# Finer regions in the kernel's own order planner: quarters of the inverse's tiles, halves of stored and output weights, single table columns

## The chip, the cores and the metric

The kernel runs on one core of a Trainium2 chip. The metric is the device time of one execution in microseconds (us), as the median over several runs; lower is better.

## The reference, cut to what matters

One layer of a decoder trunk works on 4096 positions of width 1024. The input is normalised (RMSNorm) and multiplied by one input projection. Its columns feed two groups of heads: four heads of gated linear attention, and eight heads of RWKV-7 time mixing with a delta rule. Both outputs are gated, concatenated to 1024 columns, multiplied by an output projection, added to the input and normalised again. The step that matters here is the recurrence of the RWKV heads:

```python
sa = jnp.einsum('bhvk,bhk->bhv', S, -kk_t)
S = (S * w_t[:, :, None, :]
     + sa[..., None] * (kk_t * a_t)[:, :, None, :]
     + v_t[..., None] * k_t[:, :, None, :])
y = jnp.einsum('bhvk,bhk->bhv', S, r_t)
```

The kernel does it in chunks of 64 positions. Within a chunk each position depends on all earlier ones, so each chunk and head needs the inverse of a unit triangular 64x64 matrix.

## The kernel before, in words

**Tiling.** The 4096 positions are cut into 8 blocks of 512. For each block the kernel projects the normalised input tile by tile (29 weight tiles of 1024x128, each kept as a high and a low fp16 half, three products per tile), does the two head groups, and then the output projection (8 more weight tiles). The weights are split into their halves on the chip at the start and stored to DRAM (`wdr`, one tensor for each of the 37 tiles); later blocks load the halves again with `get_w` (L612).

**A unit.** The RWKV heads go in pairs: 4 pairs by 8 blocks are 32 units, numbered 0 to 31. `rwkv_ab` (L862) prepares a unit. It writes the masked triangular matrices into the tile `Nb` (VectorE, COPY_PREDICATED), and then inverts the 32x32 diagonal blocks of all chunks and heads at once. Their rows have to be laid out differently for that, so they go through DRAM twice, by copies on SP's queue: four copies `nd<-Nb` (one for each 32 partitions of `Nb`), four copies `f<-nd` (each fetches the whole of `nd` into another 32 partitions of the tile `f`, named `f4` in the code), then 31 steps of two TENSOR_TENSOR each that build the inverse in `Tc` (on GpSimd; on VectorE for unit 31 alone), four copies `td<-Tc`, and four copies `Nb<-td`, each into the 32x32 blocks of one quarter of `Nb`. `rwkv_i` (L1012) then transposes blocks of `Nb` into `Ta` and completes the 64x64 inverse with TensorE. `rwkv_c` (L1034) is the serial chain over the 8 chunks, three dependent matmul pairs each (`ch<-sv,DD`, `ch<-us,Nb`, `ch<-uv,bk`). `out_last` (L1306) is the output projection of the last block.

**What sets the order.** The kernel writes its program order itself. Every instruction is first recorded as a `Step` with a modelled duration (`put`, L223), and the order in which the streams of work hand in their steps comes from a first running estimate (`account`, L169). `parts` (L105) says which regions an operand covers for estimated times, `whole` (L203) which regions it covers for the edges between steps. If two steps touch a region with the same key, a write after a write, a read after a write or a write after a read makes an edge, and mostly a delay too. A copy that writes a region another copy has just written is therefore modelled as starting after that one has landed. Before the change a DRAM tensor is one region, an on-chip tile is two (partitions 0 to 63 and 64 to 127), and a table of scalars (`scl`, `invs`, `pkt` and others) is one. `forward` (L264) and `backward` (L332) then schedule the steps as lists, for five pairs of parameters ten times each, and the program is written out in the order of the schedule with the shortest modelled end. Each engine, and SP with its copies, executes its instructions in that order. The semaphores are put in afterwards by the framework, from the real addresses and not from these keys.

The edges of a copy come from these lines of `put`:

```python
if k in wlast:
    s.follow(wlast[k], got(wlast[k]) if timed and eng != "T" else None)
for m in readers.get(k, ()):
    s.follow(m, (0.95 + SPARE if m.eng == "D" else 0.1) if timed else None)
```

Of the kernel before, what the change touches and what calls it, by code (L numbers as in the profile page):

```python
# [11 lines left out]
F16 = mybir.dt.float16  # L12
# [6 lines left out]
DRAM = bass.MemoryType.DRAM  # L19

P = 128
DM = 1024
KT = 8
# [23 lines left out]
NC = TB // C  # L47
# [34 lines left out]
def hymba_kernel(ctx, tc, xT, wt, wg, wo, wua, gup, pk, ck, out):  # L82
# [14 lines left out]


    TABLES = ("pkt", "scl", "invs", "hinv", "mu_s", "omu_s", "carry", "wosc", "woinv", "gnh", "lnh")
    HEADS, XS = set(), set()  # L100
    now = [0.0]
    streams = []
    ready, used, busy = {}, {}, {}

    def parts(ap):  # L105
        if ap.tensor.name == out.tensor.name or ap.tensor.name.rsplit("_", 1)[0] in TABLES:
            return []
        if ap.space == DRAM:
            return [(ap.tensor.name, 0)]
        a = ap.start_partition()  # L110
        hs = range(a // 64, (a + ap.shape[0] - 1) // 64 + 1)
        if ap.tensor.name in HEADS:
            o = ap.offset % P // 64
            e = range(2) if ap.ap[-1][1] > 64 else range(o, o + 1)
            return [(ap.tensor.name, h, i) for h in hs for i in e]
        if ap.tensor.name in XS:
            o = ap.offset % (4 * TB) // TB
            e = range(o, o + max(1, math.prod(ap.shape[1:]) // TB)) if ap.dtype == F16 else range(4)
            return [(ap.tensor.name, h, 2 + i) for h in hs for i in e]
        return [(ap.tensor.name, h) for h in hs]  # L120
# [48 lines left out]
    def account(eng, out, ins, d, lag, cols=0, tiles=None):  # L169
        rdy = lambda k: (lambda r: r[0] + early(r[1], eng))(ready.get(k, (0.0, "")))  # L170
        t = max([0.0] + [rdy(k) for a in ins for k in parts(a)]
                + [used.get(k, 0.0) for k in parts(out)]
                + [rdy(k) for k in parts(out) if eng != "T"])
        if eng == "T":
            t0, d = array.put(max(t, now[0]), d, cols, tiles)
            t, now[0] = t0, array.free
        else:
            if eng == "D":
                t0 = place("H", t, 0.5)
                t = t0 + 1.15  # L180
            t = place(eng, t, d)
            if eng != "D":
                t0 = t
        for a in ins:
            for k in parts(a):
                used[k] = max(used.get(k, 0.0), t + d + (0.95 if eng == "D" else 0.1))
        for k in parts(out):
            ready[k] = (t + d + lag, eng)
        return t0
# [13 lines left out]
    def whole(ap):  # L203
        if ap.tensor.name == out.tensor.name:
            return []
        if ap.tensor.name.rsplit("_", 1)[0] in TABLES or ap.space == DRAM:
            return [(ap.tensor.name, 0)]
        return parts(ap)

    class Step:  # L210
# [12 lines left out]
    def put(t0, eng, d, lag, cols, tiles, tab, outs, ins, f):  # L223

        keys = lambda aps: {k: k in {y for x in aps for y in parts(x)} for a in aps for k in whole(a)}
        ki, ko = keys(ins), keys(outs)
        for k in list(ki) + list(ko):
# [250 lines left out]
    def sb(pool, shape, dt, tag, bufs=1):  # L478

        key = (tag, dt)  # L480
        if key not in ring:
            ring[key] = [0, [pool.tile(shape, dt, tag=f"{tag}_{i}", name=f"{tag}_{i}") for i in range(bufs)]]
        r = ring[key]
        t = r[1][r[0] % len(r[1])]
        r[0] += 1
        return t
# [32 lines left out]
    for g in range(4):  # L519
        q = slice(32 * g, 32 * g + 32)  # L520
# [38 lines left out]
    Nb = [sb(un, [P, NC, 192], F32, f"Nb{i}") for i in range(NBUF)]  # L559
# [37 lines left out]
    wdr = [dr.tile([2, P, KT, P], F16, tag=f"wdr{i}", name=f"wdr{i}") for i in range(NWT + KT)]  # L597
# [987 lines left out]
```

## Time and profile before

| what | value |
|---|---|
| median of 3 runs | 2355.93 us (2353.73 to 2357.6) |
| the profiled execution's own time | 2350.84 us |
| its span, from the first to the last instruction | 2348.7 us |
| TensorE busy | 2230.6 us |
| VectorE, ScalarE, GpSimd busy | 1715.9, 1257.4, 865.6 us |
| mean granted TensorE clock | 0.982 |
| GpSimd waiting for the copies `f<-nd` | 468.1 us |

PE is TensorE, DVE is VectorE, ACT is ScalarE, POOL is GpSimd, SP is SyncE, whose queue (SPq) issues the copies. Nearly every instruction is put down to L438, the planner's helper that writes it out, so groups are told apart by their tiles: `bank<-x,wr` is a matmul that writes a PSUM bank from the tiles `x` and `wr`. The rows of a timeline give start, duration, engine, operation, tiles, how many instructions were merged, and in brackets how long the engine had been idle and what ended that. The wait lists give the engine with what it was about to do, what it waited for, the total in us, how many times, and the longest. The table of windows gives for each stretch its length, then busy time and instructions of PE, PEld (weight loads), DVE, ACT and POOL, the granted clock, the DMA engines' busy share and GB/s.

### The profile page before, as it was taken

What the parts mean: (1) busy time and instruction counts of PE and PEld (TensorE: products, weight loads), DVE (VectorE), ACT (ScalarE), POOL (GpSimd) and SP (SyncE); (2) the same over time, 40 slices, a digit from 0 to 9 for tenths busy, and PEclk for the clock granted to TensorE, in tenths of its full rate; (3) what the DMA queues carried; (4) which work ended last, traced back from release to release, by engine and by line L of the source; (5) the groups of instructions that cost most, each with busy time, mean ns of one, the idle gap of its engine ahead of it and who ended that gap; (6) DMA issues with size and microseconds to landing.
All of it is one profiled execution on the core that took longest, in us unless ns stands there. A gap on an engine that the chain in (4) does not pass through costs nothing.

```text
span 2348.7 us, 52029 instructions
## 1 busy us (share of the span) xinstructions
PE 2230.6 (95%) x19304; PEld 1365.0 (58%) x19304; DVE 1715.9 (73%) x3801; ACT 1257.4 (54%) x3229; POOL 865.6 (37%) x2212
## 2 busy tenths in 40 slices
PE   6998999899999999999999999999999999999976
PEld 2555565456665557556575556655575565755643
DVE  7977778568773886849776687748867487766756
ACT  7557765345643646545654556446464555544442
POOL 2442333524334153444524253341524446241300
PEclk9988999999999999999999999999999999999989
DMA  5685645354334642445434543346424464344432
GB/s 183 199 267 167 187 151 151 93 175 139 111 105 128 191 147 74 127 128 188 131 92 124 184 145 109 106 127 192 148 76 128 121 193 121 98 119 123 123 96 75
DMA packets 275362, 325.41 MB, mean 139 GB/s; under 512 B 131572, under 2 KB 132772, under 8 KB 275108
## 3 DMA queue, kind: packets, MB, share of 16 engines
q1 hardware_dynamic: 275108, 322.10, 45.5%
q8 instruction: 151, 2.47, 0.4%
q14 instruction: 103, 0.84, 0.1%
HBM read 276.94 MB, written 45.05 MB: 137 GB/s over the span
## 4 chain that ended last, share of the span: by engine, by line
PE 72%; DVE 14%; DMA 7%; ACT 4%; issue 2%; SPq 1%; POOL 0%; DVEq 0%; ACTq 0%; POOLq 0%
PE bank L438 63%; PE ch L438 7%; PE y L438 3%; DVE DD L438 1%; DMA wg<-wdr 1%; SPq L438 1%; DVE bk L438 1%; DVE x L438 1%; DMA rn<-bcda 1%; DVE nta L438 1%; DMA xr<-in_xT_dram 1%; ACT wo L438 1%; DVE Nb L438 1%; DMA wdr<-wo 1%; DVE mgr L438 1%
## 5 line engine op out<-in xcount | busy, mean ns | idle before, releaser
L438 PE MATMUL bank<-x,wr 128*128 128x512 f16 x3264 | 795.7, 381 | 13.3 <-DVE SC L438 4.7
L438 POOL TENSOR_TENSOR tm<-Tc,f 128x60 f32<-128x60 f32 (+24 forms) x961 | 338.3, 352 | 583.1 <-DMA f<-nd 468.1
L438 PEld LDWEIGHTS <-wr 128*128 128x128 f16 x3264 | 314.1, 100 | 314.7 <-issue 25.6
L438 POOL TENSOR_TENSOR Tc<-Tc,tm 128x60 f32<-128x60 f32 (+24 forms) x961 | 356.7, 371 | 74.6
L438 PE MATMUL bank<-x,wg 128*128 128x512 f16 x1536 | 376.9, 381 | 1.9 <-ACT bk L438 1.2
L438 PE MATMUL bank<-x,wo 128*128 128x512 f16 x1488 | 364.2, 382 | 2.2 <-DMA wr<-wdr 0.8
L438 DVE SCALAR_TENSOR_TENSOR sv<-ch,PC,psd 64x64 f32<-64x64 f32 x448 | 126.5, 282 | 217.2 <-PE ch L438 212.1
L438 POOL TENSOR_TENSOR xacc<-xacc,xr 128x512 f32<-128x512 f32 x98 | 132.7, 1354 | 344.2 <-ACT xr L438 229.5
L438 PEld LDWEIGHTS <-wg 128*128 128x128 f16 x1536 | 147.7, 100 | 149.3 <-issue 8.1
L438 PEld LDWEIGHTS <-wo 128*128 128x128 f16 x1488 | 146.2, 101 | 133.5 <-issue 4.9
L438 PE MATMUL bank<-wg,x 128*128 128x128 f16 x3072 | 197.5, 222 | 12.4 <-DMA wg<-wdr 12.3
L438 PEld LDWEIGHTS <-x 128*128 128x128 f16 x3120 | 189.6, 100 | 32.3 <-issue 20.0
L438 ACT ACTIVATE psd<-sv,PC 128x128 f32<-128x128 f32 x256 | 102.3, 400 | 180.7 <-DVE sv L438 135.2
L438 ACT COPY uv<-ch 64x64 f32<-64x64 f32 x512 | 105.8, 207 | 106.7 <-PE ch L438 100.8
L438 POOL MEMSET Tc<- 32x8 f32 (+1 forms) x160 | 23.6, 148 | 360.1 <-DMA td<-Tc 312.2
L438 ACT COPY us<-ch 64x64 f32<-64x64 f32 x512 | 105.5, 206 | 91.7 <-PE ch L438 83.5
L438 PEld LDWEIGHTS ch<-sv,DD 128*128 128x128 f32 x512 | 91.5, 192 | 41.4 <-DVE sv L438 14.9
L438 PEld LDWEIGHTS ch<-uv,bk 128*128 128x128 f32 x512 | 91.1, 192 | 41.5 <-ACT uv L438 16.1
L438 PEld LDWEIGHTS ch<-us,Nb 128*128 128x128 f32 x512 | 88.6, 192 | 44.7 <-ACT us L438 21.5
L438 ACT ACTIVATE sa<-bank,mu_s 128x512 f32<-128x512 f32 x104 | 71.6, 688 | 75.1 <-PE bank L438 74.3
L438 PE MATMUL ch<-uv,bk 128*128 128x128 f32 x512 | 105.8, 289 | 5.5 <-ACT uv L438 5.2
L438 PE MATMUL ch<-sv,DD 128*128 128x128 f32 x512 | 105.2, 288 | 4.9 <-DVE sv L438 4.7
(333 smaller groups left out, 3681.7 us busy)
## 6 DMA issues: line engine op xcount, KB each, us to landing
wr<-wdr SPq DMA_DIRECT2D x256, 256.0 KB
wg<-wdr SPq DMA_DIRECT2D x184, 256.0 KB
xr<-in_xT_dram SPq DMA_DIRECT2D x176, 256.0 KB
wo<-wdr SPq DMA_DIRECT2D x128, 256.0 KB
f<-nd SPq DMA_DIRECT2D x128, 128.0 KB
x<-in_wt_dram SPq DMA_DIRECT2D x29, 512.0 KB
wdr<-wo SPq DMA_DIRECT2D x25, 512.0 KB
out_dram<-mgg SPq DMA_DIRECT2D x33, 256.0 KB
```

The source lines that it names most:

```text
L438: put(t0, self.name, d, lag, cols, tiles, tab, outs, ins, lambda: f(*a, **kw))
```

## The change

The change edits only the two functions that give regions their keys. No instruction is added or removed by it, and no operand or tile changes; the edges and delays that the planner works with do.

- `dram`, new, splits three kinds of DRAM tensor. `nd` has four regions: a copy `nd<-Nb` touches one, a copy `f<-nd` all four. `td` has four: a copy `td<-Tc` touches one, a copy `Nb<-td` all four. Each `wdr` has two, the high and the low half of a weight.
- `FINE` gives `Nb` a region for every 32 partitions and `f` one for every 16, in place of one for every 64. So the four copies into `f` no longer share a key, and neither do the four into `Nb`.
- The tile `wo` (the output weights, and the staging tile of the weight split) gets a region for each half, when an fp16 operand touches one half only.
- `whole` gives a table one region for each column in place of one for the table.

```diff
+    FINE = {"Nb": 32, "f": 16}
...
+    def dram(ap):
+
+        name = ap.tensor.name
+        if name.startswith("nd"):
+            return [(name, i) for i in (range(4) if ap.shape[0] == 32 and len(ap.shape) == 2 else [ap.offset // (NC * 1024) % 4])]
+        if name.startswith("td"):
+            return [(name, i) for i in (range(4) if ap.ap[0][0] >= 1024 else [ap.offset // 1024 % 4])]
+        if name.startswith("wdr"):
+            return [(name, i) for i in ([ap.offset // (P * DM) % 2] if ap.ap[0][1] == P and len(ap.shape) == 3 and ap.shape[1] == KT and ap.shape[2] == P else range(2))]
+        return [(name, 0)]
+
     def parts(ap):
         if ap.tensor.name == out.tensor.name or ap.tensor.name.rsplit("_", 1)[0] in TABLES:
             return []
         if ap.space == DRAM:
-            return [(ap.tensor.name, 0)]
+            return dram(ap)
         a = ap.start_partition()
+        tag = ap.tensor.name.rsplit("_", 1)[0].rstrip("0123456789_")
+        if tag in FINE:
+            q = FINE[tag]
+            return [(ap.tensor.name, h) for h in range(a // q, (a + ap.shape[0] - 1) // q + 1)]
         hs = range(a // 64, (a + ap.shape[0] - 1) // 64 + 1)
+        if tag == "wo":
+            o = ap.offset // DM % 2
+            e = range(o, o + 1) if ap.dtype == F16 and ap.ap[1][0] < DM else range(2)
+            return [(ap.tensor.name, h, i) for h in hs for i in e]
...
     def whole(ap):
...
-        if ap.tensor.name.rsplit("_", 1)[0] in TABLES or ap.space == DRAM:
-            return [(ap.tensor.name, 0)]
+        if ap.space == DRAM:
+            return dram(ap)
+        if ap.tensor.name.rsplit("_", 1)[0] in TABLES:
+            w = math.prod(ap.tensor.shape[1:])
+            return [(ap.tensor.name, i) for i in range(ap.offset % w, ap.offset % w + math.prod(ap.shape[1:]))]
         return parts(ap)
```

## The prediction

> **What bounds the kernel now.** I read the page first, then a table of windows, then the waits of PE by window, and last the timelines of the place where the waits are.
>
> ```profile
> PE 2230.6 (95%) x19304; PEld 1365.0 (58%) x19304; DVE 1715.9 (73%) x3801; ACT 1257.4 (54%) x3229; POOL 865.6 (37%) x2212
> ...
> PE   6998999899999999999999999999999999999976
> ```
>
> PE is the bound, and its tenths are below 9 almost only in the first and the last slices. The windows say how much is lost where:
>
> ```profile
> 0.00:235.00 235.00, 194.63 (x1527) 116.04 (x1528) 190.72 (x528) 153.50 (x297) 84.93 (x178) 0.93 0.65 204
> 235.00:470.00 235.00, 219.14 (x1813) 132.05 (x1811) 172.28 (x393) 136.30 (x369) 91.62 (x266) 0.98 0.49 146
> 470.00:2232.00 1762.00, 1732.96 (x15264) 1067.09 (x15263) 1280.36 (x2680) 926.41 (x2444) 688.31 (x1763) 1.00 0.44 132
> 2232.00:2349.00 117.00, 83.85 (x707) 49.84 (x705) 72.49 (x201) 41.17 (x121) 0.74 (x5) 0.88 0.30 86
> ```
>
> The second number after the stretch is PE's busy time. PE is idle for 40.4 us of the first 235, 15.9 us of the next, 29.0 us of the long middle (98.4% busy there) and 33.2 us of the last 117. An edit that changes only the order can win no more than these idle times, and the time that the lower clock (0.93 and 0.88, the column before the last two) costs beside them. The waits of PE, first for the tail, then for the stretch from 235 to 2232, then for the head:
>
> ```profile
> PE bank L438 <- DVE Ta L438: 12.3, 3, 11.5
> ```
>
> ```profile
> PE bank L438 <- DMA wg<-wdr: 12.8, 7, 3.6
> ...
> PE bank L438 <- DVE Ta L438: 2.0, 3, 0.8
> ```
>
> ```profile
> PE ch L438 <- ACT uv L438: 3.1, 4, 1.5
> PE ch L438 <- DVE sv L438: 2.8, 5, 0.7
> ...
> PE ch L438 <- ACT us L438: 1.9, 3, 1.1
> ```
>
> One wait stands out: 11.5 us in the tail for `Ta`, the transposed blocks of the inverse that `rwkv_i` takes from `Nb`. The timelines of PE, DVE and SP show it:
>
> ```profile
> 2252.30 0.31 PE L438 MATMUL bank<-Ta,Nb 32*32 32x32 f32 x2 [11.54 <-DVE Ta L438]
> ```
>
> ```profile
> 2241.01 0.19 DVE L438 TENSOR_TENSOR tm<-Tc,f 128x31 f32<-128x31 f32 x1
> ...
> 2251.82 0.42 DVE L438 STREAM_TRANSPOSE Ta<-Nb 32x256 f32<-32x256 f32 x1
> ...
> 2256.98 0.17 DVE L438 TENSOR_TENSOR Tc<-Tc,tm 128x8 f32<-128x8 f32 x1
> ...
> 2274.37 0.90 DVE L438 STREAM_TRANSPOSE Ta<-Nb 32x256 f32<-32x256 f32 x2
> ```
>
> ```profile
> 2219.84 2.18 SPq L438 DMA_DIRECT2D nd<-Nb  x4
> 2223.52 0.30 SPq L438 DMA_DIRECT2D td<-Tc  x1
> ...
> 2231.46 0.31 SPq L438 DMA_DIRECT2D f<-nd  x1
> 2231.83 0.41 SPq L438 DMA_DIRECT2D td<-Tc  x1
> 2232.28 0.45 SPq L438 DMA_DIRECT2D f<-nd  x1
> ...
> 2233.72 0.42 SPq L438 DMA_DIRECT2D td<-Tc  x1
> 2234.20 0.90 SPq L438 DMA_DIRECT2D f<-nd  x2
> ...
> 2237.99 0.46 SPq L438 DMA_DIRECT2D td<-Tc  x1
> ...
> 2241.36 1.02 SPq L438 DMA_DIRECT2D Nb<-td  x2
> ...
> 2244.45 0.96 SPq L438 DMA_DIRECT2D Nb<-td  x2
> ...
> 2257.22 1.80 SPq L438 DMA_DIRECT2D td<-Tc  x4
> ```
>
> Two units are in flight. The `td` copies from 2223.5 to 2238.0, the `Nb` copies and the transposes at 2251.8 belong to unit 30; the `nd` and `f` copies and the VectorE steps from 2241.0 to 2257.2 to unit 31, the last. Unit 30's inverse was there at 2223.5, when its first `td` copy went out, but the fourth went out 14.5 us later. That is the planner's doing: four copies with one key are planned each after the last has landed, and SP takes what the plan put between. The chip asks for no such thing. At 2257.22 four `td` copies go out in 1.80 us, and at 2219.84 four `nd` copies in 2.18 us, less than one copy's way to DRAM and back (3.4 us and more from the last `td` issue at 2237.99 to the first `Nb` copy). The real semaphores know the quarters already.
>
> **The change part by part.** No instruction is added or removed, so busy times stay; what can move is idle time.
>
> *Quarters of `nd`, `td`, `f` and `Nb`, the tail.* For unit 30 the last `td` copy moves from 2238.0 to 2223.5 + 3/4 of 1.80 = 2224.9, 13.1 us earlier, and two more us are won where the `Nb` copies no longer go in spaced pairs (2241.36 to 2245.42 is 4.1 us, four in a row about 2.0). `Ta` then comes at about 2251.8 - 15 = 2237, ahead of the end of PE's work at 2252.3 - 11.5 = 2240.8. The whole wait of 11.5 us goes. What is late next is unit 31: its chain follows unit 30's. Its transposes stand at 2274.4, 17 us after its inverse ended at 2257.2. Its `f` copies can go out some 3.4 us after 2222.0, at 2225.4 where the first now goes at 2231.5, so 6 us earlier; the VectorE steps need 16 us, and behind them four `td` and four `Nb` copies take 1.80 + 3.4 + 2.0 = 7.2 us to issue; with 6.4 us from the last `Nb` issue to `Ta` (2245.4 to 2251.8 for unit 30) that is 13.6 in place of 17.2. So unit 31 moves by 6 + 3.6 = 10 us if VectorE starts as soon as `f` allows, and by up to 15 if the plan also takes out the gap ahead of 2241.0. PE is not idle through all of that: behind the wait it runs at a lower clock.
>
> ```profile
> 2232.00:2252.00 20.00, 8.76 (x49) 4.04 (x47) 13.34 (x51) 3.30 (x8) 0.74 (x5) 0.85 0.55 130
> 2252.00:2290.00 38.00, 34.48 (x340) 22.93 (x341) 21.14 (x63) 20.40 (x63) 0.00 (x0) 0.86 0.28 80
> ```
>
> 38 us at 0.86 lose 5.3 us at the most. The tail is therefore worth 10 us (unit 31 is late next) to 17 us (wait and clock both gone); I take 12, near the wait itself.
>
> *The same, the head.* Unit 0 shows the same spread, here by its first `td` copy, its last one, and POOL's wait until it could clear `Tc` for the next unit:
>
> ```profile
> 139.48 0.48 SPq L438 DMA_DIRECT2D td<-Tc  x1
> ...
> 153.50 0.43 SPq L438 DMA_DIRECT2D td<-Tc  x1
> ```
>
> ```profile
> 158.72 0.90 POOL L438 MEMSET Tc<- 128x256 f32 x5 [24.66 <-DMA td<-Tc]
> ```
>
> About 12 us go from that chain. What PE lost to the first chains are the three waits of `ch` above, 7.8 us. DVE is busy for 190.7 of the 235 us there with the weight split, so an earlier chain may only find PE idle at another time. Between 0 and 8 us, I take 3.
>
> *The same, the middle.* POOL's waits for `f` and `td` shrink there too, but POOL has time to spare. PE's 29 us of idle time over 1762 hold hardly any wait for the inverse (2.0 us for `Ta` above). The order is worked out anew as a whole, and its effect here isn't known. The trace bounds it by its own stretches of 235 us, the worst and the best of the middle:
>
> ```profile
> 470.00:705.00 235.00, 229.16 (x2094) 144.42 (x2093) 180.34 (x375) 126.00 (x328) 85.05 (x212) 0.99 0.44 132
> ...
> 1645.00:1880.00 235.00, 233.34 (x2074) 141.22 (x2071) 163.63 (x355) 124.07 (x324) 101.63 (x275) 1.00 0.41 118
> ```
>
> With 7.5 stretches like the best (1.66 us idle) the middle has 12.4 us idle in place of 29, a gain of 17; with all like the worst (5.84) 43.8, a loss of 15. I take 0, as it stands.
>
> *Halves of `wdr` and `wo`, columns of the tables.* The loads of the two output halves need no longer be planned one after the other, but in no window is a wait of PE for them among the rows that matter; the large one is for `wg`, whose halves are tiles of their own already. Cover: the loads go out a projection ahead; without it each could cost what a wait for `wg` costs, 12.8 / 7 = 1.8 us. The stored halves and the columns matter while the weights are split, where they only allow other orders. I take 0 for these, and the bounds are those of the head (0 to -8, and as much the other way, since a worse order costs what a better one wins).
>
> *A rule that speaks against packing.* The trace gives 3.4 us from the last spread `td` issue to the first `Nb` copy. By the Trainium skill (DMA: Bandwidth & Descriptors, Queues, rings and completion order) the write that signals a copy's end lands only behind every earlier write of the same DMA engine, also of other queues; a packed group behind large loads would then be signalled later. No row here separates that. If it cost each of unit 30's and unit 31's second round trips one more us, the tail would be worth 10 instead of 12.
>
> *Sum.* -12 - 3 + 0 + 0 = -15 us against the profiled execution: 2350.84 - 15 = 2335.8. That execution is 5.1 us below the median of the runs shown, so for the median 2355.9 - 15 = **2341 us**.
>
> **Rivals.**
>
> *A. More of the same.* Tail 17, head 8: 2355.9 - 25 = 2331 us. For it speaks the clock of 0.86; against it unit 31, which is late next, and the busy VectorE of the head.
>
> *B. No change.* The tail's gain is given back: unit 31's inverse on VectorE isn't moved, since the last block's other VectorE work stands ahead of 2241.0, or the middle loses as much as the tail wins. A mere 0 to 4 us remains: 2354 us. That the edit doesn't act at all is part of this, but the four-fold copies above are all planned by the keys it splits.
>
> *C. Packed copies hold up weight loads (slower).* SP issues in order. Today weight loads stand between the spread copies; four packed copies are 1.8 us of issue, and the first copy of the next group waits for the last of the one before, with the loads behind it in the queue. In the middle, at 98.4% busy, PE has no slack for a late weight, and `wg<-wdr` is its largest wait already: 1.8 us a time. One more such wait in every second unit is 16 x 1.8 = 29 us, less the 15: 2370 us. It decides from 9 more waits on (15 / 1.8 = 8.3). Against it: a load goes out when its buffer is free, a projection ahead, and packed groups let SP go sooner.
>
> **How the numbers follow.** This kernel's measurement can tell about 0.2%, 4.7 us, from no change. Chances: forecast (2331 to 2350) 0.45, A 0.12, B 0.10, C 0.33. Faster is the forecast and A, 0.57; the same is B, 0.10; slower is C, 0.33. The range goes from the forecast with the middle's best (2341 - 15 = 2326) to C as priced, 2370; below it lies a small part of A, above it some two fifths of C (more late weights than one in every second unit). The forecast's own range is 2331 to 2350.
>
> **What would show it.** POOL's wait for the `td` copies, over the whole run, is the sum that the spread makes:
>
> ```profile
> POOL Tc L438 <- DMA td<-Tc: 312.2, 24, 24.7
> ```
>
> Right: `nd`, `f`, `td`, `Nb` copies of one unit go out in fours within about 2 us; PE's wait of 11.5 us for `Ta` after 2240 is gone and the window of the last 117 us has some 12 us less idle time; POOL's total wait for `td<-Tc` (312 us) falls by a third or more; the middle's PE share stays near 98.4%. Wrong: the copies are still spread, or PE's waits for `wg<-wdr` and `wr<-wdr` grow above some 28 us (C), or the middle's idle time grows by more than the tail's shrinks.

## The result, and the profile after

The changed kernel takes 2329.2 us (median of 4 runs, 2324.2 to 2333.7), the kernel before 2356.8 us (median of 4). The ratio is 0.988, with a 95% interval of 0.986 to 0.991: faster by 27.5 us, where 15 were forecast. The profiled execution took 2324.2 us, with a span of 2322.4; the one of before 2350.84 and 2348.7. The profiled execution of one kernel further down (the kernel before with the constant 0.44) ran in a slow state, at a mean granted clock of 0.56, so only the times of its other runs are used.

The work is the same; what has moved is where PE stands idle and how fast its clock runs. Here is the first part of the page of the kernel after:

```profile
PE 2221.9 (96%) x19304; PEld 1368.5 (59%) x19304; DVE 1720.4 (74%) x3801; ACT 1246.0 (54%) x3229; POOL 878.7 (38%) x2212
```

PE's busy time falls by 8.7 us although it has the same 19304 matmuls; a part of that is the mean granted clock, which rose from 0.982 to 0.985. The copies did what was expected. This is SP's timeline of the kernel after for the last two units:

```profile
2191.85 2.38 SPq L461 DMA_DIRECT2D td<-Tc  x4
...
2195.58 1.94 SPq L461 DMA_DIRECT2D Nb<-td  x4
2200.28 1.78 SPq L461 DMA_DIRECT2D nd<-Nb  x4
2203.40 1.71 SPq L461 DMA_DIRECT2D f<-nd  x4
...
2229.62 1.84 SPq L461 DMA_DIRECT2D td<-Tc  x4
...
2233.92 1.78 SPq L461 DMA_DIRECT2D Nb<-td  x4
```

Each group of four goes out in about 2 us here; over all units most do, though half of the `nd` groups still take longer, up to 7.9 us. Unit 30's way back (`td` to the last `Nb`) takes 5.7 us where it took 21.9. Over the 32 units, from SP's whole timeline, the median way out (first `nd` issue to the end of the last `f` issue) falls from 16.2 to 7.2 us, the median way back from 15.6 to 6.6. In the waits of the whole run, POOL waits less than half as long for `td`, and more for `f`, since it now comes back earlier and stands idle ahead of its next unit instead:

```profile
POOL tm L461 <- DMA f<-nd: 675.1, 30, 48.9
POOL Tc L461 <- DMA td<-Tc: 139.4, 30, 15.6
```

**Where the time came from.** The two tables of windows, of before and then of after, have the same stretches at the start, and the last 117 us of each span at the end:

```profile
0.00:118.00 118.00, 92.45 (x664) 50.81 (x666) 97.31 (x273) 77.26 (x138) 43.11 (x72) 0.96 0.60 190
118.00:235.00 117.00, 102.19 (x867) 65.23 (x866) 93.42 (x256) 76.24 (x160) 41.82 (x107) 0.89 0.70 218
...
2231.70:2348.70 117.00, 84.15 (x708) 49.99 (x706) 72.49 (x201) 41.17 (x122) 0.74 (x5) 0.88 0.30 86
```

```profile
0.00:118.00 118.00, 91.54 (x664) 51.57 (x664) 98.05 (x273) 79.13 (x141) 50.26 (x85) 0.97 0.64 203
118.00:235.00 117.00, 109.08 (x955) 69.09 (x952) 102.93 (x277) 81.58 (x179) 40.60 (x116) 0.98 0.74 225
235.00:470.00 235.00, 225.83 (x1963) 138.25 (x1961) 171.35 (x405) 138.13 (x375) 95.18 (x254) 1.00 0.52 151
470.00:2205.40 1735.40, 1702.91 (x15001) 1055.26 (x15003) 1273.50 (x2640) 904.25 (x2411) 692.65 (x1759) 0.99 0.46 133
2205.40:2322.40 117.00, 92.58 (x738) 54.34 (x732) 74.56 (x208) 42.86 (x126) 0.00 (x0) 0.85 0.28 82
```

A stretch costs PE its idle time, and at most (1 - clock) x length for running slowly; I call the sum the lost time. It counts the time twice in which PE idles at the low clock, so it is an upper estimate. From 118 to 235 us before lost 14.8 + 12.9 = 27.7 us, after 7.9 + 2.3 = 10.3. Over the first 470 us (the row from 235 to 470 of before stands in the prediction) it is 78.5 before and 49.4 after: 29 us won, give or take 2 for the rounding of the clock. With the low clock counted only where PE is busy, from the trace's own record of the clock, it is 23 us. By 470 us the kernel after has done 3582 matmuls, the kernel before 3344. The last 117 us lost 46.9 before and 42.0 after: 5 us won, by either count. The span is 26.3 shorter, so the middle lost some 8 us.

**The head, seen closer.** Unit 0's way back, in SP's timelines of before (its first `td` copy, at 139.48, stands in the prediction) and then of after, and the first link of its chain that needs the inverse, in PE's timelines of both:

```profile
161.67 1.32 SPq L438 DMA_DIRECT2D Nb<-td  x2
```

```profile
130.99 1.94 SPq L461 DMA_DIRECT2D td<-Tc  x4
...
135.82 1.85 SPq L461 DMA_DIRECT2D Nb<-td  x4
```

```profile
172.07 0.33 PE L438 MATMUL ch<-us,Nb 128*128 128x64 f32 x2
```

```profile
143.94 0.33 PE L461 MATMUL ch<-us,Nb 128*128 128x64 f32 x2
```

The `nd` copies of unit 0 start at the same time in both (80.2 and 80.5 us), but this link comes 28 us earlier: 8 us are won on the way out up to the start of the inverse (101.25 and 93.69 us), and 20 between the first `td` copy and the first matmul on `Ta` (28.8 us before, 8.4 after). The windows of before, while the chain of unit 0 ran, and of after, for the same chain and then the same time:

```profile
176.00:205.00 29.00, 20.81 (x114) 13.06 (x114) 21.07 (x60) 26.57 (x64) 13.31 (x28) 0.76 0.64 197
```

```profile
186.00:191.00 5.00, 2.81 (x13) 1.58 (x11) 4.38 (x10) 4.69 (x13) 4.29 (x10) 1.00 0.00 0
191.00:204.70 13.70, 8.48 (x46) 6.25 (x46) 8.03 (x33) 13.04 (x35) 0.35 (x2) 0.50 0.72 221
```

```profile
143.00:176.00 33.00, 30.07 (x183) 16.87 (x184) 27.05 (x77) 27.12 (x60) 18.46 (x51) 1.00 0.83 260
176.00:205.00 29.00, 25.13 (x333) 18.41 (x333) 25.52 (x68) 23.24 (x58) 0.74 (x5) 1.00 0.76 221
```

Before, the first chain came late, at 172 us, and from 186 us on PE had little else left to do. PE stood idle between the links, and from 191 to 204.7 us the granted clock was 0.50 (the 0.76 is the mean with the 1.00 ahead of it). There the links took twice as long, as these two matmuls of PE's timeline of before show:

```profile
182.09 0.39 PE L438 MATMUL ch<-uv,bk 128*128 128x128 f32 x2
...
192.64 0.80 PE L438 MATMUL ch<-uv,bk 128*128 128x128 f32 x2 [1.52 <-ACT uv L438]
```

After, the chain starts at 144 us, among projections, and the clock stays at 1.00.

**The tail, seen closer.** The wait of 11.5 us for `Ta` is gone. What came in its place is in PE's timeline of after and the window around it:

```profile
2223.70 0.43 PE L461 MATMUL ch<-us,Nb 128*128 128x64 f32 x2 [0.93 <-ACT us L461]
...
2230.00 0.80 PE L461 MATMUL ch<-sv,DD 128*128 128x128 f32 x2 [0.84 <-DVE sv L461]
...
2234.86 0.80 PE L461 MATMUL ch<-uv,bk 128*128 128x128 f32 x2 [2.79 <-ACT uv L461]
...
2240.21 1.49 PE L461 MATMUL bank<-x,wo 128*128 128x512 f16 x3
```

```profile
2222.00:2240.00 18.00, 10.19 (x63) 7.36 (x62) 14.76 (x45) 9.76 (x33) 0.00 (x0) 0.61 0.41 88
```

Unit 30's chain now runs earlier, but alone. The output projection that could fill its gaps (`bank<-x,wo`) comes at 2240, behind the scaling of the last block. These 18 us lose 7.8 of idle time and at most 7.0 of clock. It is a bare chain in place of a bare wait.

The chain could have gone on 12 us sooner, while PE still had projections to do. Its first three matmul pairs are done on PE at 2209.7, but VectorE's next step for it (`sv<-ch`) comes only at 2221.5, behind the steps of unit 31's inverse, which VectorE runs from 2209.7 on:

```profile
2209.28 0.38 PE L461 MATMUL ch<-uv,bk 128*128 128x128 f32 x2
```

```profile
2209.72 0.19 DVE L461 TENSOR_TENSOR tm<-Tc,f 128x31 f32<-128x31 f32 x1
...
2221.53 0.27 DVE L461 SCALAR_TENSOR_TENSOR sv<-ch,PC,psd 64x64 f32<-64x64 f32 x1
```

### The profile page after: what moved, and what is told of

Same layout as the page of the kernel before. It is cut to its first block, busy times and chain, and to the rows that moved or that the text cites. A ratio compares the mean times of both kernels' runs of the same rounds, so it can differ in the third digit from the quotient of the medians.

```text
span 2322.4 us, 52066 instructions
## 1 busy us (share of the span) xinstructions
PE 2221.9 (96%) x19304; PEld 1368.5 (59%) x19304; DVE 1720.4 (74%) x3801; ACT 1246.0 (54%) x3229; POOL 878.7 (38%) x2212
## 4 chain that ended last, share of the span: by engine, by line
PE 67%; DVE 16%; DMA 8%; ACT 4%; issue 2%; SPq 2%; POOL 0%; DVEq 0%; ACTq 0%; POOLq 0%
PE bank L461 58%; PE ch L461 6%; PE y L461 3%; SPq L461 2%; DMA xr<-in_xT_dram 2%; DVE DD L461 2%; DVE nta L461 1%; DMA wdr<-wo 1%; DVE x L461 1%; DVE Nb L461 1%; DVE bk L461 1%; DVE mgr L461 1%; DVE xr L461 1%; DVE mgg L461 1%; DMA rn<-bcda 1%
## 5 line engine op out<-in xcount | busy, mean ns | idle before, releaser
L461 POOL TENSOR_TENSOR tm<-Tc,f 128x60 f32<-128x60 f32 (+24 forms) x961 | 352.4, 367 | 758.3 <-DMA f<-nd 675.1
L461 POOL TENSOR_TENSOR Tc<-Tc,tm 128x60 f32<-128x60 f32 (+24 forms) x961 | 351.0, 365 | 74.4
L461 PEld LDWEIGHTS <-x 128*128 128x128 f16 x3120 | 189.8, 100 | 24.2 <-issue 12.9
L461 PEld LDWEIGHTS ch<-sv,DD 128*128 128x128 f32 x512 | 92.2, 192 | 40.1 <-DVE sv L461 10.8
L461 PE MATMUL ch<-us,Nb 128*128 128x64 f32 x512 | 91.4, 260 | 8.2 <-ACT us L461 8.0
```

Of the source, the lines that this page charges most:

```text
L461: put(t0, self.name, d, lag, cols, tiles, tab, outs, ins, lambda: f(*a, **kw))
```

## The experiments

Three theories. **Q**: shorter round trips of the inverse, as the planner sees them, carry the gain. **H**: the halves and columns carry it, by freeing the weight split at the start. **L**: luck, any new order would move as far. Later runs then ask where and by what the quarters act. Ratios are against the kernel before, with 95% intervals.

**The quarters alone.** The `wdr` branch of `dram`, the `wo` branch of `parts` and the columns in `whole` are taken out:

```diff
-        if name.startswith("wdr"):
...
-        if tag == "wo":
...
-            w = math.prod(ap.tensor.shape[1:])
+            return [(ap.tensor.name, 0)]
```

> Only nd, td, f and Nb get the finer regions; wdr, wo and the tables stay as before. Theory Q (the round trips of the inverse carry the gain): most of the 27 us is here, 2325 to 2337 us, with the first 470 us holding some 12 us less idle PE time than before. Rival H (the halves and the columns free the weight split at the start): little, 2348 to 2357 us. Rival L (any new order would do as well or as badly): anywhere from 2330 to 2370.

2319.1 us, 0.983 (0.981 to 0.986), below the whole change and 6 us below what Q had named. Q holds in that the gain is here, but the head's share is smaller than Q said it would be: the first 470 us lost 71 us (before 78.5) with 9.5 us less idle time, the last 117 lost 36 (before 47). H falls.

**The rest alone**, with the coarse keys of `nd`, `td`, `f` and `Nb`:

```diff
-    FINE = {"Nb": 32, "f": 16}
+    FINE = {}
...
-        if name.startswith("nd"):
...
-        if name.startswith("td"):
```

> Only the halves of wdr and wo and the columns of the tables; nd, td, f and Nb stay as before. Theory Q: 2350 to 2361 us, as before, and the copies of one unit stay spread. Rival H: 2328 to 2340 us, with the gain in the first 470 us. Rival L: anywhere from 2330 to 2370.

2363.9 us, 1.003 (1.001 to 1.005): a little slower than before, 3 us above what Q had named. The copies stay spread. H falls a second time.

**How far an order moves by itself.** One constant of the planner, 10 ns, in the kernel before and in the changed one:

```diff
-SPARE = 0.45
+SPARE = 0.46
```

> The kernel before with one planner constant moved by 10 ns (SPARE 0.45 to 0.46), which changes no region but has the whole order worked out anew; this measures how far an order moves by itself. Theories Q and H: within 8 us of 2356.5 (2348 to 2364). Rival L: more than 12 us away from it on either side.

> The changed kernel with the same constant moved (SPARE 0.46). Theories Q and H: within 8 us of 2329 (2321 to 2337), so the two kernels with the fine regions lie apart from the two without. Rival L: the four overlap, this one at 2340 or more.

2368.1 us, 1.005 (1.003 to 1.007), for the kernel before; 2314.4 us, 0.982 (0.980 to 0.984), for the changed one. Both moved by more than the 8 us I had allowed, in opposite directions: a new order is worth some 12 to 15 us either way. The two kinds still lie far apart. Two more, to have more orders of each kind, the quarters alone with 0.46 and the kernel before with 0.44:

> The quarters alone with SPARE 0.46. Theory Q: 2310 to 2330 us, so that four orders worked out with quarters (2329, 2319, 2314 and this) lie below all orders without. If the halves and columns are worth something of their own, this lies above 2314 (the changed kernel with SPARE 0.46) by more than 5 us; if they cost, below it by as much.

> The kernel before with SPARE 0.44, another new order with coarse regions. Theory Q: 2346 to 2372 us. Rival L (luck of the order): below 2335 us.

2325.2 us, 0.987 (0.986 to 0.989), and 2363.3 us, 1.003 (1.002 to 1.004). With quarters in all units there are now four orders, at 2314, 2319, 2325 and 2329; without quarters there are four as well (rest, before, and before with either constant), at 2356, 2363, 2364 and 2368. L falls as an account of the gain. With 0.46 the whole change is 11 us faster than the quarters alone, with 0.45 it is 10 us slower, so what halves and columns are worth on their own can't be told from this.

**Where the quarters act.** A flag makes a copy or a block operation cover the coarse regions again in all units but the chosen ones (first 0 to 5 and the setup, then 6 to 31, then 30 and 31); `wdr`, `wo` and the tables stay coarse:

```diff
+        fine[0] = u < 6
...
             q, e = FINE[tag], a + ap.shape[0]
+            if not fine[0]:
+                a, e = a // 64 * 64, (e + 63) // 64 * 64
```

> Quarters (nd, td, f, Nb) as in the run with the quarters alone, but only for units 0 to 5 and the setup; every later unit covers its regions as coarsely as before. Theory Head (the gain is made in the first 470 us, where the first chains wait for the round trips): 2328 to 2345 us, with 3500 or more matmuls done by 470 us (before: 3344, the changed kernel 3582). Rival Tail (the term my prediction named): 2350 to 2362 us. A new order alone moves up to 12 us.

> Quarters only from unit 6 on. Theory Head: 2336 to 2352 us, since the tail gives its part and the middle little, and about 3340 matmuls by 470 us. Rival Tail: 2325 to 2340 us, nearly all of the gain.

> Quarters only for the last two units, 30 and 31. By the prediction's tail term: 12 us off, 2340 to 2350 us, PE's wait of 11.5 us for Ta after 2240 gone. Theory Head: 4 to 12 us off, 2344 to 2353 us. If the tail is worth nothing: 2356 or more.

Units 0 to 5: 2350.2 us, 0.998 (0.996 to 0.999). Units 6 to 31: 2361.9 us, 1.002 (1.000 to 1.003). Units 30 and 31: 2349.1 us, 0.997 (0.995 to 0.998). By the medians theory Head fails twice: the first lies in the range that Rival Tail had named, and the second lies 10 us above Head's and further above Tail's. The third lies where both the tail term and Head had put it, and in its trace PE's wait for `Ta` after 2240 is gone. The windows say where the time went. First the run with units 0 to 5:

```profile
0.00:118.00 118.00, 94.19 (x664) 53.00 (x665) 98.75 (x270) 77.19 (x135) 48.11 (x83) 0.95 0.65 201
118.00:235.00 117.00, 113.04 (x994) 72.17 (x993) 103.81 (x290) 87.89 (x196) 46.52 (x124) 0.98 0.75 231
235.00:470.00 235.00, 223.41 (x1890) 138.13 (x1889) 165.94 (x387) 131.47 (x359) 87.10 (x246) 0.96 0.48 143
470.00:2229.50 1759.50, 1723.43 (x15047) 1054.11 (x15046) 1265.28 (x2655) 913.77 (x2418) 683.37 (x1760) 0.99 0.45 131
```

The head is as good as forecast: 3548 matmuls by 470 us, 57 us lost where before lost 78.5. The middle gives it back: of the 22 us that the table below puts down to it, 7 are idle time (36 us in place of 29) and 3 are clock (by the trace's own record; the rows above have it too coarsely). The other 12 are in neither, and stay open. Now the run with units 30 and 31, its end:

```profile
2230.10:2347.10 117.00, 92.73 (x775) 54.33 (x774) 77.48 (x215) 44.13 (x128) 0.00 (x0) 0.89 0.29 85
```

37 us lost in the last 117, where before lost 47: this is the tail term alone, some 10 us, and the whole run is 7 to 8 us faster. The same sums for all other runs that have a profile to compare, with the middle as what is left of the span's difference, follow in us won against before (minus is lost). These are single profiled executions, some us off the medians, and the clock's rounding makes the first column uncertain by 2. The middle is rougher still: PE's busy time less (1 - clock) x span, which should be the same in every run if idle time and clock were all, is 2180 to 2200 us.

| run | first 470 us | last 117 us | middle | span |
|---|---|---|---|---|
| the change | 29 | 5 | -8 | 26 |
| quarters alone | 7 | 11 | 10 | 28 |
| the change, SPARE 0.46 | 28 | 13 | -2 | 39 |
| quarters alone, SPARE 0.46 | 22 | 11 | -7 | 26 |
| units 0 to 5 | 21 | 3 | -22 | 2 |
| units 6 to 31 | -14 | 15 | -10 | -9 |
| units 30 and 31 | -1 | 10 | -7 | 2 |
| rest alone | -6 | 5 | -16 | -17 |
| before, SPARE 0.46 | 0 | -6 | -7 | -13 |
| copies packed, order kept (below) | -9 | -2 | -22 | -33 |
| quarters of `td` and `Nb` (below) | 21 | 14 | -14 | 20 |
| quarters of `nd` and `f` (below) | 12 | 7 | -26 | -7 |

Head and tail follow the quarters: every run that has them in the early units wins 7 to 29 us at the start, where the others have -14 to 0; every run that has them in the last two wins 5 to 15 at the end, where the others have -6 to 5. (These two ranges touch at 5, so the tail is less certain than the head.) The start of unit 0's chain parts the runs as well: its first `ch<-us,Nb` comes at 140 to 160 us in the seven runs with quarters in the early units, at 172 to 184 in the six without. An early start alone doesn't set the gain: with the quarters alone it is at 150 us and the head wins 7, with those of `td` and `Nb` at 160 and it wins 21. The middle follows nothing that I can name: the kernel before has one of the best middles of all, and all orders but one lose 2 to 26 us there. That is where the partial runs give their gains back; why is open.

**Copies packed, order kept.** The coarse order is worked out, and then only the four copies of each kind and unit are put side by side on SP:

```diff
+        for kind in (("nd", "Nb"), ("f", "nd"), ("td", "Tc"), ("Nb", "td")):
+            four = [s for s in steps if s.kind == kind]
...
+                j = at[q[-1 if kind[0] == "nd" else 0].n][0]
```

> The kernel before, its order worked out with the coarse regions, and only then the four copies of each kind and unit are put next to each other on SP's queue (nd at the last one's place, f, td and Nb at the first one's). Every other engine keeps its order. Theory Plan (the gain comes from the order of all engines, worked out with shorter round trips): 2345 to 2360 us. Rival Copies (the data arrive earlier, and that is the gain): 2320 to 2338 us.

2377.1 us, 1.009 (1.007 to 1.011): slower by 20 us, outside what either theory named. Plan holds in that packing without a new order gains nothing, but has no account of the loss. Copies isn't fully tested: the median way out fell as with the quarters (16.2 to 6.1 us), but the way back only from 15.6 to 13.5, since the `Nb` copies stay at the place that the coarse order gave the first of them. SP's, PE's and VectorE's timelines of this run, at the place of the old wait:

```profile
2254.48 1.88 SPq L439 DMA_DIRECT2D td<-Tc  x4
...
2273.68 2.06 SPq L439 DMA_DIRECT2D Nb<-td  x4
```

```profile
2285.18 0.31 PE L439 MATMUL bank<-Ta,Nb 32*32 32x32 f32 x2 [11.54 <-DVE Ta L439]
```

```profile
2273.88 0.19 DVE L439 TENSOR_TENSOR tm<-Tc,f 128x31 f32<-128x31 f32 x1
...
2284.70 0.42 DVE L439 STREAM_TRANSPOSE Ta<-Nb 32x256 f32<-32x256 f32 x1
```

The `td` copies go out in 1.9 us, and the wait is there as before, to the hundredth of a microsecond: the `Nb` copies stand behind other entries of SP's queue, 17 us later, and the transposes stand at their old place in VectorE's order. That place sets the wait. In both runs the transposes stand in the middle of unit 31's inverse, 10.8 us behind its first step (2273.88 to 2284.70 here, 2241.01 to 2251.82 before), and VectorE doesn't stand idle in between. This is the step just ahead of them in the kernel before:

```profile
2251.68 0.22 DVE L438 TENSOR_TENSOR tm<-Tc,f 128x60 f32<-128x60 f32 x1
```

The last `Nb` copy had gone out by 2245.4 there, 6 us earlier. So PE's old wait didn't end on the copies but on VectorE, whose order had been planned for late copies. With quarters for units 30 and 31 the transposes come at 2229.7, ahead of unit 31's inverse, which starts at 2236.8. Data that arrive early are no use when the consumer's place was planned late. Why the run is slower still is open: PE's idle time is 17 us longer over the span and its clock is lower (span's mean 0.974, before 0.982), but no single wait explains 20 us.

**The way out or the way back.** The quarters for `td` and `Nb` only, then for `nd` and `f` only:

```diff
-    FINE = {"Nb": 32, "f": 16}
+    FINE = {"Nb": 32}
...
-        if name.startswith("nd"):
```

> Quarters for the way back only (td and Nb); nd and f stay coarse, as do wdr, wo and the tables. Theory Whole (what counts is the length of the whole round trip, about half of it on either side, in every unit): half of the gain of the quarters, 2332 to 2345 us. Theory Back (the td copies hold Tc, and with it the next unit's inverse on POOL, so the way back is what matters): 2315 to 2328 us. A new order alone moves up to 12 us.

> Quarters for the way out only (nd and f); td and Nb stay coarse. Theory Whole: 2332 to 2345 us. Theory Back: 2346 to 2360 us, near the kernel before, and POOL's wait for the td copies stays near 300 us.

2329.8 us, 0.989 (0.987 to 0.990), and 2347.5 us, 0.997 (0.995 to 0.998). The way back alone brings as much as the whole change; the way out alone 8 us, within what an order moves. The waits of POOL for `Tc`, of the first run and then of the second:

```profile
  POOL Tc L452: 168.5, 29
```

```profile
  POOL Tc L452: 330.0, 23
```

This is theory Back's sign: the `td` copies hold `Tc`, and with it POOL's next unit. The times fit theory Back better than Whole, since each run shortens its own way by the same 9 us in the median (back to 6.7 us, out to 6.9). But 2330 lies between Back's 2315 to 2328 and Whole's 2332 to 2345, and the difference of the two runs, 18 us, is not far beyond the scatter of orders. The sign is no proof either: with quarters from unit 6 on, POOL's wait for `td` fell to 192 us, and that run won nothing. And unit 0's chain starts 12 us earlier in the first run and 17 in the second, which is nearer to Whole. Which of the two ways counts more is open.

## Why the prediction was right, step by step

The direction and the range were right (2326 to 2370, measured 2329.2), and the forecast's 15 us was 12 short. The cause was the one named, shorter round trips in the plan; the terms of the sum were not where I put them. That the time falls inside the range is partly luck: it lies 2 us below the forecast's own range (2331 to 2350), and the wider one reaches down to 2326 only for a best case of the middle, which lost time instead, while the head won what no term had.

- *The copies of a unit go out in fours, POOL's wait for `td` falls by a third or more:* right in the main, 312 to 139 us, and 5.7 us for unit 30's way back; half of the `nd` groups took more than 2.6 us.
- *Tail, 12 us:* the wait for `Ta` went as predicted, but not by the step named. The 6.4 us from the last `Nb` issue to `Ta` were read as the copies' way; they were VectorE's order (above), and in the kernel after unit 31's two transposes start 0.8 and 2.3 us behind the end of the last `Nb` issue (2236.52 and 2237.99, behind 2235.70). Earlier copies helped because the plan then put the transposes ahead of unit 31's inverse. The profiled tail won only 5. Unit 31 was to move by 10 to 15 us; the first of its transposes came at 2236.5, 38 us earlier than before, but 12 counted from the end of each span, and PE took them up without a wait. Late next was unit 30's chain, held on VectorE by unit 31's inverse for 12 us and then left without the output projection beside it, at a clock of 0.61. In the other three orders with quarters everywhere the tail was worth 11 to 13, so the size was about right and this order's tail a poor one.
- *Head, 3 us, between 0 and 8:* this step failed. Measured 29 (23 with the low clock counted only where PE is busy), and 7 to 28 in the other three orders. It let unit 0's chain move by 12 us, the spread of its `td` copies alone, where it moved by 28. It counted the three waits of the chain as all that PE lost to it, and left out the clock, though the row for the head showed 0.93 and I had priced the clock in the tail: from 118 to 235 us alone the clock cost up to 12.9 us and idling 14.8. It also ended the head at 235 us; the 15.9 us of idle time up to 470 were read out and given to no term.
- *Middle, 0, with -15 to +17 as bounds:* -8 here, +10 to -8 in the four orders with quarters. The bounds held for these four; other orders went past them, to -26.
- *Halves and columns, 0:* alone 8 us slower, which is within the scatter of orders.
- *Rival B* (given back in the tail) happened in part. *Rival C* (packed copies hold up weight loads) did not: PE's waits for `wg<-wdr` fell from 12.8 to 3.0 us, as the row below from the kernel after shows. *Rival A's* 2331 us was near the time, but with 17 + 8 in place of 5 + 29.

```profile
PE bank L461 <- DMA wg<-wdr: 3.0, 5, 0.8
```

- *The rule of the Trainium skill* (DMA: Bandwidth & Descriptors, Queues, rings and completion order: a copy's signal lands behind earlier writes of its DMA engine) can't be priced here. From the start of the last `td` issue to the first `Nb` copy it was 3.4 us when spread, but SP issued five other copies in that time (of `x<-wdr` and `bv<-bcdb`, between 2238.64 and 2241.26), so this was no copy's way, and the term of 3.4 us in the prediction was too long. Packed it is 2.0 us for unit 30 (2191.85 + 3/4 of 2.38 = 2193.6, to 2195.58) and 2.9 for unit 31 (2231.0 to 2233.92); what makes the 0.9 us between them isn't shown.

## What to carry to other kernels

When an order is planned by a model, look for accesses that the model holds to conflict and the chip does not: copies issued far apart in one place and back to back in another are the sign. Free the plan, not only the queue, since an early transfer helps only if its consumer was planned for it. And price a stretch with gaps by its idle time plus at most (1 - clock) x length; from 118 to 235 us here the clock cost nearly as much as the gaps. Before a change to a planner is believed at 1%, perturb it: here 10 ns on a constant moved the kernel by 0.5%.

## What the runs showed of the hardware that was not expected

- Gaps of 0.2 to 0.7 us between the links of a chain came just ahead of a fall of PE's granted clock: in the kernel before PE was 56% busy from 186 to 191 us, and the clock was 0.50 for the next 13.7 us. In the kernel after, 18 us with PE 57% busy had a mean of 0.61, while 33 us at 91% busy ran at 1.00. At the low clock `ch<-uv,bk` took 0.80 us in place of 0.39.
- Packing the copies on SP's queue, with every other engine's order kept, made the kernel slower by 0.9% (0.7 to 1.1%).
